# Causal masks of the prompt attention added by products of the rounded fp32 type in place of bf16 ones

## The chip, the cores and the metric

One core of a Trainium2 chip runs the whole kernel in one launch. The metric is the device time in microseconds, from which the median of several runs is taken; lower is better. The engines are TensorE (PE in the profile, its loads of stationary operands PEld), VectorE (DVE), ScalarE (ACT), GpSimd (POOL) and SyncE (SP), which issues most DMAs.

## The reference, cut to what matters

One layer of a decoder is computed for a prompt of 1024 tokens and for 8 sequences of 8 new tokens each, which attend to 8192 cached positions. A layer has gated linear attention, latent attention, an output projection, a gated MLP with a short convolution, and a gated embedding. The change lies in the prompt's part of the latent attention, with 8 heads of 96 (64 of values):

```python
def prompt_attention(q, k, v):           # q, k: (1, 1024, 8, 96); v: (1, 1024, 8, 64)
    ...
        s = jnp.einsum('bqhd,bkhd->bhqk', qi, k, preferred_element_type=jnp.float32) * MLA_SCALE
        qpos = start + jnp.arange(Q_BLOCK)
        s = jnp.where(kpos[None, :] <= qpos[:, None], s, NEG)      # NEG = -1e30
        pr = jax.nn.softmax(s, axis=-1)
        return jnp.einsum('bhqk,bkhd->bqhd', pr.astype(v.dtype), v)
```

## The kernel before, in words

Arithmetic is kept close to fp32 by splitting an operand into two of a rounded fp32 type (`F32R` in the code, `fp32r` or `f32` in the profile): a high part and the rest. A product is then the sum of three matmuls, high by high, high by low and low by high (`mm3`, L139 to L141).

Two streams of work share the core for the first half of the span. The cache stream (tiles `ks`, `csq`, `css`, `sn`, `phl`, `cpv`, `ctp`, `crp`, `chl`) reads the cached latents of the 8 sequences in blocks and does the new tokens' attention. The dense stream does the prompt: projections, linear attention, then `prompt_attention`, then the output projection. Generators yield shares of work, and a loop takes from the one or the other by a fixed table of paces. Within that, a scheduler sets the order of the instructions on each engine at build time from its own estimates of their durations, so a change of one instruction's type can move its neighbours; each engine then runs its list strictly in order. Buffers of a pool (three PSUM banks with the tag `d` here) are handed out in that order too.

`prompt_attention` goes through 16 rounds, one for each head `h` and half `g` of 512 queries. A round has two parts, and the second part of one round runs beside the first part of the next:

- `prepare` transposes and splits q and k of a head (`operands`, L1263), then `shifts` computes for each tile of 128 queries the scores against all keys up to the diagonal with the high parts alone (L1279, tile `t`), adds the mask to the 128 columns on the diagonal (L1281), and VectorE takes each row's maximum (L1282, `amx`). The negated maxima are transposed (L1292) into row 96 of `qh` and `ql`, which meets a row of ones in `kh`.
- `values` computes the scores transposed, 128 keys by up to 512 queries (tile `S`, three matmuls L1308, L1309, L1312), with a mask (L1311) where the keys are in the same half as the queries. There the tile has 512, 384, 256 or 128 columns. ScalarE takes the exponential (`p`), it is split (`ph`, `pl`, the rest on GpSimd, L1318), and three matmuls (L1323, L1324, L1326, at the end L1330) sum the values and the denominators in `o`.

A mask is a matmul: the identity as the stationary operand, a 128x128 matrix of 0 and -1e30 as the moving one, added to the scores that are in PSUM. `identb`, `maskq` and `maskk` are bf16, and are made once on GpSimd at the stage's start (L1240 to L1246). The 16 rounds have 4 tiles with a mask of each kind, so 64 matmuls at L1281 and 64 at L1311. A matmul with bf16 operands appears as a separate weight load and a matmul in the built program; one with operands of the rounded type is one instruction there, and the profile shows both halves in either case.

Of the kernel before, what the change touches and what calls it, by code (L numbers as in the profile page):

```python
# [8 lines left out]
F32 = mybir.dt.float32  # L9
F32R = mybir.dt.float32r  # L10
BF16 = mybir.dt.bfloat16
I32 = mybir.dt.int32
AF = mybir.ActivationFunctionType
ALU = mybir.AluOpType
# [4 lines left out]
P = 128  # L19
# [16 lines left out]
NEG = -1e30  # L36
# [8 lines left out]
def step_kernel(ctx: ExitStack, tc: tile.TileContext, A):  # L45
    nc = tc.nc
    pe, act, dve, pool, sp = nc.tensor, nc.scalar, nc.vector, nc.gpsimd, nc.sync
# [4 lines left out]
    def ctile(shape, dt, name):  # L52
        return const.tile(shape, dt, name=name, tag=name)
# [3 lines left out]
    ident = ctile([P, P], F32, "ident")  # L57
# [131 lines left out]
    def pat(kind):  # L189
        return psD.tile([P, 512], F32, tag="d", name=kind)  # L190
# [24 lines left out]
    for i in range(2):  # L215
        for s in range(2):
# [5 lines left out]
                       pattern=[[0, 8], [1, 8]], compare_op=ALU.is_ge, fill=NEG, base=0, channel_multiplier=-1)  # L222
# [1003 lines left out]
    def prompt_attention(ap):  # L1226
# [3 lines left out]
        def load(h):  # L1230
            ld = {}
            for nm, src, w in (("q", dq, 96), ("k", dk, 96), ("v", dv, 64)):
                t_ = ap.tile([P, NT, w], F32, tag="ld" + nm, name="ld" + nm, bufs=1)
                sp.dma_start(t_, src[:, h * w:(h + 1) * w].rearrange("(t p) c -> p t c", p=P))
                ld[nm] = t_
            return ld

        ld = {0: load(0)}
        identb = ap.tile([P, P], BF16, name="identb", tag="identb", bufs=1)
        pool.tensor_copy(identb, ident)  # L1240
        masks = []
        for nm, sg in (("maskq", 1), ("maskk", -1)):
            m = ap.tile([P, P], BF16, name=nm, tag=nm, bufs=1)
            pool.memset(m, 0.0)
            pool.affine_select(m, m, pattern=[[-sg, P]], compare_op=ALU.is_ge, fill=NEG, base=0, channel_multiplier=sg)
            masks.append(m)  # L1246
        maskq, maskk = masks
        qk, vo = [], []
# [20 lines left out]
        def shifts(h, g):  # L1269
            tr = qk[h % 2]  # L1270
            mx = ap.tile([P, 4, 2], F32, tag="amx", name="amx")
            for ii in range(4):
                i = 4 * g + ii
                qs = slice(i * P, (i + 1) * P)
                for j in range(g + 1):
                    kw = (ii + 1) * P if j == g else 512
                    S = pat("t")
                    k0 = j * 512
                    pe.matmul(S[:, 0:kw], tr["qh"][0:96, qs], tr["kh"][0:96, k0:k0 + kw], start=True, stop=j < g)  # L1279
                    if j == g:  # L1280
                        pe.matmul(S[:, kw - P:kw], identb, maskq, start=False, stop=True)  # L1281
                    dve.tensor_reduce(mx[:, ii, j:j + 1], S[:, 0:kw], AX.X, ALU.max, negate=True)  # L1282
                yield 0.06 * (i + 1)
            if g == 1:
                dve.tensor_tensor(mx[:, :, 0], mx[:, :, 0], mx[:, :, 1], ALU.min)
            return mx
# [9 lines left out]
        def values(h, g):  # L1296
            tr = qk[h % 2]
            v = vo[h % 2]
            o = pat("o")
            nj = 4 * g + 4  # L1300
            pls, q = {}, []
            for j in range(nj + 1):
                if j < nj:
                    c0 = max(0, j - 4 * g) * P
                    ks = slice(j * P, (j + 1) * P)
                    qs = slice(g * 512 + c0, g * 512 + 512)
                    S = pat("S")
                    pe.matmul(S[:, c0:], tr["kh"][:, ks], tr["qh"][:, qs], start=True, stop=False)  # L1308
                    pe.matmul(S[:, c0:], tr["kh"][:, ks], tr["ql"][:, qs], start=False, stop=False)  # L1309
                    if j >= 4 * g:  # L1310
                        pe.matmul(S[:, c0:c0 + P], identb, maskk, start=False, stop=False)  # L1311
                    pe.matmul(S[:, c0:], tr["kl"][:, ks], tr["qh"][:, qs], start=False, stop=True)  # L1312
                    p = ap.tile([P, 512], F32, tag="p", name="p", bufs=3)
                    ph = ap.tile([P, 512], F32R, tag="ph", name="ph", bufs=3)
                    pl = ap.tile([P, 512], F32R, tag="pl" if j else "pl0", name="pl", bufs=3 if j else 2)
                    act.activation(p[:, c0:], S[:, c0:], AF.Exp)
                    (dve.tensor_copy if j % 2 else act.copy)(ph[:, c0:], p[:, c0:])  # L1317
                    pool.tensor_tensor(pl[:, c0:], p[:, c0:], ph[:, c0:].bitcast(F32), ALU.subtract)  # L1318
                    q.append((j, c0, ph, pl))
                    yield 0.65  # L1320
                if j > 0:
                    jj, c0, ph, pl = q.pop(0)
                    pe.matmul(o[:, c0:], v[:, jj, 0:128], ph[:, c0:], start=jj == 0, stop=False)  # L1323
                    pe.matmul(o[0:64, c0:], v[:, jj, 128:192], ph[:, c0:], start=False, stop=False)  # L1324
                    if jj > 0:
                        pe.matmul(o[:, c0:], v[:, jj, 0:128], pl[:, c0:], start=False, stop=False)  # L1326
                    else:
                        pl0 = pl
                    yield 0.6
            pe.matmul(o, v[:, 0, 0:128], pl0, start=False, stop=True)  # L1330
            r = ap.tile([64, 512], F32, tag="ar", name="ar")
            act.activation(r, o[64:128, :], AF.Ln)
            act.activation(r, r, AF.Exp, scale=-1.0)
            dve.tensor_tensor(r, o[0:64, :], r, ALU.mult)
            sp.dma_start(doT[512 + h * 64:512 + (h + 1) * 64, g * 512:(g + 1) * 512], r)
            yield 0.2
# [10 lines left out]
        def prepare(n):  # L1347
            h, g = divmod(n, 2)
            if g == 0:
                yield from operands(h, ld.pop(h))  # L1350
                if h + 1 < H:
                    ld[h + 1] = load(h + 1)
            mx = yield from shifts(h, g)
            rows(h, g, mx)

        yield from prepare(0)
        for n in range(2 * H):
            yield from both(values(*divmod(n, 2)), prepare(n + 1) if n + 1 < 2 * H else iter(()))
# [904 lines left out]
```

## Time and profile before

| | |
|---|---|
| median of 3 runs | 2215.05 us (2214.86 to 2217.98) |
| span of the profiled execution, first to last instruction | 2211.1 us, mean granted clock 0.988 |
| own time of the profiled execution | not given apart; the runs' median lies 3.95 us over the span |
| PE busy | 2126.7 us, 96% |
| PEld, DVE, ACT, POOL busy | 87%, 75%, 62%, 56% |
| stage of the prompt attention | 645 to 1060 us of the span |

Busy times are unions of the instructions' spans. Matmuls are pipelined: a new one starts while the one before drains, so their durations overlap, and the throughput is read from the starts in the timeline. In the rows of groups the fields are line, engine, operation, out<-in, shape of the stationary operand, of the moving one, count, busy us and mean ns, and the idle time before them with what ended it.

### The profile page before, as it was taken

The page shows a single profiled execution, that of the slowest core. Times are in us where ns is not written, and L with a number is a line of the kernel's source. Part 1 is how long each engine was busy: PE and PEld are TensorE (multiplying, and loading weights), DVE is VectorE, ACT ScalarE, POOL GpSimd, SP SyncE. Part 2 cuts the span into 40 slices and gives each one's busy share as a digit, 9 for nine tenths or more (in the row PEclk, how much of TensorE's full clock was granted, in tenths as well). Part 3 has the DMA queues.
Part 4 walks back from the last instruction along what each step waited for, and adds up shares of the span by engine and source line. Part 5 has one row for each costly group of instructions (what it writes and reads, how often), then busy time and mean ns, then how long its engine had stood idle before and what let it go on. Part 6 is the DMA issues. An engine that isn't in the chain of part 4 may idle for free.

```text
span 2211.1 us, 38379 instructions
## 1 busy us (share of the span) xinstructions
PE 2126.7 (96%) x13460; PEld 1927.2 (87%) x13460; DVE 1668.4 (75%) x2551; ACT 1366.7 (62%) x3724; POOL 1233.9 (56%) x1330
## 2 busy tenths in 40 slices
PE   7999989999999999999999997999999999999999
PEld 6889978878888888887898875999999999888899
DVE  4775667467788888887888788888888886887642
ACT  5676766777778888887777766333333333534631
POOL 5675668576777777778455557756566562011100
PEclk9999999999999999999999998999999999999999
DMA  5343235412342222221522222332232325777321
GB/s 185 106 144 108 78 119 156 141 54 69 105 120 61 63 74 61 61 56 46 171 77 69 74 77 82 101 102 90 92 95 91 101 91 191 240 218 237 101 71 39
DMA packets 204418, 233.07 MB, mean 105 GB/s; under 512 B 42422, under 2 KB 146339, under 8 KB 204227
## 3 DMA queue, kind: packets, MB, share of 16 engines
q1 hardware_dynamic: 188259, 179.49, 26.0%
q0 software_dynamic: 14736, 46.67, 7.4%
q10 hardware_dynamic: 1232, 4.46, 0.5%
q8 instruction: 108, 1.77, 0.3%
q14 instruction: 83, 0.68, 0.1%
HBM read 188.00 MB, written 42.52 MB: 104 GB/s over the span
## 4 chain that ended last, share of the span: by engine, by line
PE 79%; DVE 7%; ACT 5%; DMA 3%; POOL 3%; issue 2%; SPq 0%; DVEq 0%; POOLq 0%; ACTq 0%
PE ps_gu L140 7%; PE ps_gu L141 7%; PE ps_gu L139 7%; PE ks L139 5%; PE ks L141 4%; PE ks L140 4%; PE ps_dn L140 3%; PE ps_dn L141 3%; PE ps_dn L139 3%; PE cpv L646 2%; PE ctp L522 2%; PE ps_lt L278 2%; PE ps_pj L139 2%; DVE css L565 1%; PE ps_pj L140 1%
## 5 line engine op out<-in xcount | busy, mean ns | idle before, releaser
L560 ACT ACTIVATE csq<-ks 128x256 f32<-128x256 f32 x1040 | 392.7, 400 | 91.1 <-PE ks L141 80.2
L565 DVE TENSOR_REDUCE css<-csq 128x16 f32<-128x1024 f32 (+1 forms) x264 | 315.7, 1196 | 61.2 <-ACT csq L560 58.2
L115 ACT CAST wh<-st 128x512 fp32r<-128x512 f32 x176 | 108.4, 619 | 189.0 <-PE ps_gu L140 168.7
L139 PE MATMUL ks<-mv0h,cTh 128*128 128x320 f32 (+1 forms) x520 | 171.0, 331 | 8.8 <-ACT sn L562 4.6
L139 PE MATMUL ks<-mv1h,cTh 128*128 128x320 f32 (+1 forms) x520 | 169.6, 328 | 7.8 <-ACT sn L562 3.5
L605 POOL TENSOR_TENSOR chl<-craw,chl 128x1024 fp32r<-128x1024 f32 x64 | 141.6, 2213 | 55.2 <-ACT chl L603 53.0
L140 PE MATMUL ks<-mv1l,cTh 128*128 128x320 f32 (+1 forms) x520 | 153.1, 296 | 0.0
L140 PE MATMUL ks<-mv0l,cTh 128*128 128x320 f32 (+1 forms) x520 | 152.0, 294 | 0.0
L141 PE MATMUL ks<-mv0h,cTl 128*128 128x320 f32 (+1 forms) x520 | 147.6, 297 | 0.9 <-DVE cTl L116 0.8
L141 PE MATMUL ks<-mv1h,cTl 128*128 128x320 f32 (+1 forms) x520 | 148.0, 298 | 0.1
L116 DVE TENSOR_TENSOR wl<-st,wh 128x512 fp32r<-128x512 f32 x132 | 119.0, 903 | 26.3 <-ACT wh L115 26.3
L631 POOL TENSOR_TENSOR phl<-sn,phl 128x512 fp32r<-128x512 f32 (+1 forms) x64 | 85.5, 1335 | 84.8 <-ACT phl L630 84.3
L116 POOL TENSOR_TENSOR wl<-st,wh 128x512 fp32r<-128x512 f32 x44 | 69.4, 1578 | 102.9 <-ACT wh L115 102.9
L140 PE MATMUL ps_dn<-o 128*128 128x512 f32 x308 | 120.1, 390 | 0.4 <-DVE o L116 0.4
L141 PE MATMUL ps_dn<-o 128*128 128x512 f32 x308 | 120.2, 390 | 0.0
L116 DVE TENSOR_TENSOR cTl<-ctp,cTh 128x512 fp32r<-128x512 f32 (+1 forms) x136 | 90.0, 662 | 37.8 <-ACT cTh L115 36.8
L139 PEld LDWEIGHTS ks<-mv0h,cTh 128*128 128x128 f32 x520 | 97.9, 188 | 23.2 <-ACT sn L562 9.4
L562 ACT COPY sn<-ks 128x64 f32<-128x64 f32 x520 | 116.7, 224 | 0.0
L139 PEld LDWEIGHTS ks<-mv1h,cTh 128*128 128x128 f32 x520 | 99.0, 190 | 20.1 <-ACT sn L562 7.9
L1318 POOL TENSOR_TENSOR pl<-p,ph 128x512 fp32r<-128x512 f32 (+1 forms) x96 | 97.5, 1020 | 30.3 <-DVE ph L1317 21.2
L139 PE MATMUL ps_dn<-o 128*128 128x512 f32 x308 | 112.1, 390 | 0.0
L141 PE MATMUL ps_gu<-xrh,wl 128*128 128x320 f32 x352 | 108.7, 309 | 0.0
(670 smaller groups left out, 7871.4 us busy)
## 6 DMA issues: line engine op xcount, KB each, us to landing
raw<-ds SPq DMA_DIRECT2D x77, 256.0 KB
raw<-ffn_w_down SPq DMA_DIRECT2D x66, 256.0 KB
stage<-w_in SPq DMA_DIRECT2D x48, 256.0 KB
st<-ffn_w_gate SPq DMA_DIRECT2D x44, 256.0 KB
st<-ffn_w_up SPq DMA_DIRECT2D x44, 256.0 KB
wr<-ffn_w_down SPq DMA_DIRECT2D x44, 256.0 KB
ds<-cv SPq DMA_DIRECT2D x21, 512.0 KB
oraw<-doT SPq DMA_DIRECT2D x16, 256.0 KB
```

The lines of the kernel that those rows point to most:

```text
L115: cast = act.copy(hi, src)
L116: res = (lo_eng or dve).tensor_tensor(lo, src, hi.bitcast(F32), ALU.subtract)
L139: pe.matmul(ps, ah, bh, start=first, stop=False)
L140: pe.matmul(ps, ah, bl, start=False, stop=False)
L141: return pe.matmul(ps, al, bh, start=False, stop=last)
L278: pe.matmul(ps, x, w, start=first, stop=last)
L560: act.activation(sq[:, f * 256:f * 256 + 256], ks[:, 0:256], AF.Square)
L562: act.copy(o.sn[:, g0 + i, :], ks[:, 256:320])
L565: dve.tensor_reduce(o.ss[:, g0 + i + 1 - n:g0 + i + 1, :].rearrange("p i h -> p (i h)"), sq2[:, :n].rearrange("p i (h n) -> p (i h) n", n= ...
L605: pool.tensor_tensor(ch[:, c0:c1, 128:256], src, ch[:, c0:c1, 0:128].bitcast(F32), ALU.subtract)
L631: pool.tensor_tensor(phl[:, :nt, 64:128], sb, phl[:, :nt, 0:64].bitcast(F32), ALU.subtract)
L1318: pool.tensor_tensor(pl[:, c0:], p[:, c0:], ph[:, c0:].bitcast(F32), ALU.subtract)
```

## The change

The identity and the two masks are kept in the rounded type. Since GpSimd's fill and selection write plain fp32, each mask is first made in a buffer `mraw` (one for both) and then cast. The two matmuls take `identr` in place of `identb`; nothing else is edited.

```diff
-        identb = ap.tile([P, P], BF16, name="identb", tag="identb", bufs=1)
-        pool.tensor_copy(identb, ident)
+        identr = ap.tile([P, P], F32R, name="identr", tag="identr", bufs=1)
+        pool.tensor_copy(identr, ident)
         masks = []
         for nm, sg in (("maskq", 1), ("maskk", -1)):
-            m = ap.tile([P, P], BF16, name=nm, tag=nm, bufs=1)
-            pool.memset(m, 0.0)
-            pool.affine_select(m, m, pattern=[[-sg, P]], compare_op=ALU.is_ge, fill=NEG, base=0, channel_multiplier=sg)
+            raw = ap.tile([P, P], F32, name="mraw", tag="mraw", bufs=1)
+            m = ap.tile([P, P], F32R, name=nm, tag=nm, bufs=1)
+            pool.memset(raw, 0.0)
+            pool.affine_select(raw, raw, pattern=[[-sg, P]], compare_op=ALU.is_ge, fill=NEG, base=0, channel_multiplier=sg)
+            pool.tensor_copy(m, raw)
             masks.append(m)
...
-                        pe.matmul(S[:, kw - P:kw], identb, maskq, start=False, stop=True)
+                        pe.matmul(S[:, kw - P:kw], identr, maskq, start=False, stop=True)
...
-                        pe.matmul(S[:, c0:c0 + P], identb, maskk, start=False, stop=False)
+                        pe.matmul(S[:, c0:c0 + P], identr, maskk, start=False, stop=False)
```

Lines behind the masks' making stand two further down in the changed kernel (L1281 is L1283, L1311 is L1313, L1312 is L1314). On every engine the order differs only within the stage of the prompt attention; behind it the same rows follow with other buffer numbers. Three places show how. On GpSimd at the start of the stage, before (the matching rows from the selections on):

```order
L473 DMA craw<-cache_ckv,idx 128x1024 x2
L1245 AFFINE_SELECT maskq<-maskq 128x128
L1245 AFFINE_SELECT maskk<-maskk 128x128
L592 TENSOR_TENSOR sn<-sn,cy 128x512
L116 TENSOR_TENSOR vo_9440<-ldv,vo_9440 128x8x64
L631 TENSOR_TENSOR phl<-sn,phl 128x9x64
L594 TENSOR_TENSOR sn<-sn,sr 128x512
L605 TENSOR_TENSOR chl<-craw,chl 128x8x128
```

and now:

```order
L1246 AFFINE_SELECT mraw<-mraw 128x128
L592 TENSOR_TENSOR sn<-sn,cy 128x512
L116 TENSOR_TENSOR vo_9444<-ldv,vo_9444 128x8x64
L631 TENSOR_TENSOR phl<-sn,phl 128x9x64
L1247 CAST maskq<-mraw 128x128
L594 TENSOR_TENSOR sn<-sn,sr 128x512
L1245 MEMSET mraw 128x128
L1246 AFFINE_SELECT mraw<-mraw 128x128
L1247 CAST maskk<-mraw 128x128
L605 TENSOR_TENSOR chl<-craw,chl 128x8x128
```

The first mask is finished behind `phl`, the second behind the `sn` that follows it, and `chl` comes behind both. On TensorE, at the first round, where `cpv` is the cache stream's product that needs `phl`, before:

```order
L646 MATMUL cpv<-chl,phl 128x258 x9
L1308 MATMUL S<-qh_9436,kh_9438 128x512
L1279 MATMUL t<-kh_9438,qh_9436 128x512
L1309 MATMUL S<-ql_9437,kh_9438 128x512
L1311 LDWEIGHTS identb
L1311 MATMUL S<-maskk,identb 128x128
L1312 MATMUL S<-qh_9436,kl_9439 128x512
```

and now:

```order
L646 MATMUL cpv<-chl,phl 128x258 x9
L1283 MATMUL t<-maskq,identr 128x128 x3
L1281 MATMUL t<-kh_9442,qh_9440 128x512
L1283 MATMUL t<-maskq,identr 128x128
L1294 MATMUL t<-ident,amx 1x128 x3
L522 MATMUL ctp<-ident,craw 128x128 x4
L500 MATMUL crp<-ident,krraw 128x128 x2
L1294 MATMUL t<-ident,amx 1x128
```

The masks of the first four score tiles, which stood ahead of `cpv`, now stand behind it, and the first tile of values starts later by these rows and six products of the cache stream. On TensorE near the stage's end, at the last but one `cpv` there, before:

```order
L1323 MATMUL o<-ph,vo_9448 128x512
L1324 MATMUL o<-ph,vo_9448 64x512
L1279 MATMUL t<-kh_9446,qh_9444 128x512
L1323 MATMUL o<-ph,vo_9448 128x384
L1324 MATMUL o<-ph,vo_9448 64x384
L1279 MATMUL t<-kh_9446,qh_9444 128x384
L1281 LDWEIGHTS identb
L1281 MATMUL t<-maskq,identb 128x128
L646 MATMUL cpv<-chl,phl 128x258 x8
L500 MATMUL crp<-ident,krraw 128x128 x2
```

and now:

```order
L1281 MATMUL t<-kh_9450,qh_9448 128x512
L1281 MATMUL t<-kh_9450,qh_9448 128x256
L1283 MATMUL t<-maskq,identr 128x128
L646 MATMUL cpv<-chl,phl 128x258 x8
L500 MATMUL crp<-ident,krraw 128x128 x2
L1325 MATMUL o<-ph,vo_9452 128x512
L1326 MATMUL o<-ph,vo_9452 64x512
L1325 MATMUL o<-ph,vo_9452 128x384
L1326 MATMUL o<-ph,vo_9452 64x384
L1281 MATMUL t<-kh_9450,qh_9448 128x512
L1281 MATMUL t<-kh_9450,qh_9448 128x384
L1283 MATMUL t<-maskq,identr 128x128
```

The `cpv` moved ahead of four products of values and a score tile.

## Prediction

> **What bounds the kernel now.** I read the page first, then the stretch in which the two masks are used, then the matmul lines by shape, and last the matmul timeline around single masks.
>
> ```profile
> PE 2126.7 (96%) x13460; PEld 1927.2 (87%) x13460; DVE 1668.4 (75%) x2551; ACT 1366.7 (62%) x3724; POOL 1233.9 (56%) x1330
> ...
> PE 79%; DVE 7%; ACT 5%; DMA 3%; POOL 3%; issue 2%; SPq 0%; DVEq 0%; POOLq 0%; ACTq 0%
> ```
> TensorE is busy for 96% of the span and holds 79% of the chain that ended last. Below, "slot" is the time from the start of one matmul to the start of the next: the durations overlap, so only slots add up.
>
> ```profile
> 645.00:1060.00 415.00, 401.40 (x2737) 350.28 (x2735) 340.20 (x552) 355.87 (x1053) 310.24 (x316) 0.99 0.24 68
> ...
> 1020.00:1030.00 10.00, 7.59 (x41) 5.94 (x40) 6.57 (x12) 4.51 (x10) 7.81 (x13) 0.85 0.06 14
> 1030.00:1040.00 10.00, 8.78 (x45) 7.04 (x45) 4.57 (x10) 7.15 (x15) 7.63 (x8) 0.84 0.26 66
> ```
> The columns are length, then busy time of PE, PEld, DVE, ACT, POOL, then the granted clock. In the stage of the masks TensorE idles for 415.00 - 401.40 = 13.6 us; 3.6 us of it lie in the 20 us at the stage's end, where the clock falls to 0.85 too. So a nanosecond on TensorE in this stage is nearly a nanosecond of time, and no other engine is near full.
>
> ```profile
> L1281 PE MATMUL t<-maskq,identb 128*128 128x128 bf16 x64 | 14.4, 230 | 0.0
> ...
> L1326 PEld LDWEIGHTS o<-pl,vo 128*128 128x128 f32 x80 | 15.4, 193 | 1.6 <-POOL pl L1318 0.7
> ...
> L1311 PEld LDWEIGHTS <-identb 128*128 128x128 bf16 x64 | 6.3, 98 | 7.6 <-issue 6.9
> ```
> There are 64 masks of scores (L1281) and 64 of values (L1311). A stationary operand of 128x128 in the rounded type loads in 193 ns, the bf16 identity in 98 ns.
>
> **The change, part by part.**
>
> *A mask between wide products.* What it costs in bf16:
>
> ```profile
> 699.10 0.40 PE L1309 MATMUL S<-ql,kh 97*128 97x512 f32 x1
> 699.34 0.23 PE L1311 MATMUL S<-maskk,identb 128*128 128x128 bf16 x1
> 699.38 0.48 PE L1312 MATMUL S<-qh,kl 97*128 97x512 f32 x1
> 699.70 0.28 PE L139 MATMUL csr<-qbd1h,kTh 128*128 128x256 f32 x1
> ```
> The mask's own slot is 0.04 us, but the wide product after it takes 0.32 us. Without a mask ahead the same line takes 0.23, in the next rows, which also hold the nearest thing to the new mask: L1326, a narrow product of the rounded type with a full stationary operand, between two wide ones.
>
> ```profile
> 889.02 0.39 PE L1312 MATMUL S<-qh,kl 97*128 97x512 f32 x1
> 889.25 0.23 PE L1326 MATMUL o<-pl,vo 128*128 128x128 f32 x1
> 889.31 0.45 PE L1330 MATMUL o<-pl,vo 128*128 128x512 f32 x1
> 889.60 0.28 PE L139 MATMUL ks<-mv0h,cTh 128*128 128x256 f32 x1
> ```
> So bf16 costs 0.04 + (0.32 - 0.23) = 0.13 us. The rounded narrow product costs its slot of 0.06 and delays L1330 to 0.29, so 0.06 + (0.29 - 0.23) = 0.12. In both types the product behind the narrow one waits for its own stationary operand, which can't load early under so short a cover. I take 0.015 us less for each mask (the rows are printed to 0.01, so between 0 and 0.02). Of the 128 masks 96 stand so: all but those of the 128-wide tiles.
>
> *A mask among narrow products.* Each of the 16 rounds (8 heads, 2 halves) has one tile of scores and one of values that is 128 wide; here the last of values, in bf16:
>
> ```profile
> 1047.31 0.23 PE L1308 MATMUL S<-qh,kh 97*128 97x128 f32 x1
> 1047.37 0.27 PE L1309 MATMUL S<-ql,kh 97*128 97x128 f32 x1
> 1047.49 0.23 PE L1311 MATMUL S<-maskk,identb 128*128 128x128 bf16 x1
> 1047.53 0.31 PE L1312 MATMUL S<-qh,kl 97*128 97x128 f32 x1
> 1047.67 0.45 PE L1326 MATMUL o<-pl,vo 128*128 128x512 f32 x1
> 1047.96 0.39 PE L1323 MATMUL o<-ph,vo 128*128 128x512 f32 x1
> ```
> From 1047.31 to 1047.96 are 0.65 us; less the wide slot of 0.23, four narrow products cost 0.42. In the rounded type alone such a row runs so:
>
> ```profile
> 1019.91 0.22 PE L1323 MATMUL o<-ph,vo 128*128 128x128 f32 x1
> 1019.97 0.22 PE L1324 MATMUL o<-ph,vo 128*64 128x128 f32 x1
> 1020.03 0.27 PE L1326 MATMUL o<-pl,vo 128*128 128x128 f32 x1
> 1020.14 0.45 PE L1330 MATMUL o<-pl,vo 128*128 128x512 f32 x1
> 1020.42 0.22 PE L1279 MATMUL t<-kh,qh 96*128 96x128 f32 x1
> ```
> L1326, whose successor needs a full stationary operand and whose predecessor was narrow, has a slot of 0.11. Four in a row are then 0.06 + 3 x 0.11 for the slots and 0.06 for the delay of the wide one behind, 0.45 in all: 0.03 us more than with the bf16 mask. I take 0.03 for all 32 such masks.
>
> Sum on TensorE: 96 x -0.015 + 32 x 0.03 = -1.44 + 0.96 = -0.5 us. The bounds: at the lower end the delay of the product behind vanishes and a mask costs its slot alone, 0.06 for 0.13, 128 x -0.07 = -9.0 us. At the upper end the slower load is not covered at all, 193 - 98 = 95 ns, 128 x 0.095 = +12.2 us. I stay at -0.5, since L1326 is the same shape, type and place as the new mask.
>
> The Trainium skill speaks against the change here: "TensorE: Matmul & The Clock Gate", section "Weight-path perf modes — Fast Weight Load (FWL) and DoubleRow", gives the fast load of stationary operands to 128-wide ones that aren't fp32, by a factor of about two as measured there. The trace agrees with that factor, 193 against 98 ns. Its section "LDWEIGHTS (loading the stationary operand)" gives columns over 1.2 for the plain load, 107 ns for 128; were each of the 128 masks to cost that in full, an estimate is 13.7 us where my rows give 128 x 0.12 = 15.4 for the wide case, and 128 x 0.13 = 16.6 for bf16 in the same rows: by the page the sum would be 13.7 - 16.6 = -2.9 us, by the rows -0.5.
>
> *Building the masks on POOL*, once:
>
> ```profile
> 647.07 0.50 POOL L1240 CAST identb<-ident 128x128 bf16<-128x128 f32 x1
> 647.52 0.20 POOL L1244 MEMSET maskq<- 128x128 bf16 x1
> ...
> 651.14 0.53 POOL L1255 MEMSET vo<- 128x512 f32 x1
> ...
> 656.52 0.31 POOL L1245 TENSOR_SCALAR_AFFINE_SELECT maskq<-maskq 128x128 bf16<-128x128 bf16 x1
> 656.79 0.29 POOL L1245 TENSOR_SCALAR_AFFINE_SELECT maskk<-maskk 128x128 bf16<-128x128 bf16 x1
> ...
> 659.35 1.40 POOL L631 TENSOR_TENSOR phl<-sn,phl 128x576 fp32r<-128x576 f32 x1
> 660.72 1.28 POOL L594 TENSOR_TENSOR sn<-sn,sr 128x512 f32<-128x512 f32 x1
> 663.24 2.19 POOL L605 TENSOR_TENSOR chl<-craw,chl 128x1024 fp32r<-128x1024 f32 x1 [1.25 <-PE S L1312]
> ```
> Two casts are added, 2 x 0.50 by L1240, whose size they have. The fills and the two selections move from 2 to 4 bytes: a fill between 0.20 and 0.53, a selection between 0.31 and twice that. Together +1.0 to +2.3 us; I take 1.3, since the cast between these types takes 0.50 whatever comes out. One buffer (mraw) serves both masks, so the second's fill waits for the first's cast on the same engine. Because maskk is now built behind phl, phl itself comes 0.20 + 0.29, about 0.5 us, earlier. Then follow maskq's cast, L594 (1.28) and maskk's three instructions (about 1.1), ahead of L605, which idled 1.25 us before it. That idle time hides them; if it is gone, L605 starts up to 0.6 us late, and who waits for it is the next block's cpv product, many matmuls later. In the new order the first scores masks stand behind cpv and the first value mask some thirty matmuls behind that, about 4 us by their slots, so TensorE waits for neither. Cost: nothing.
>
> *The moved rows.* The order in front of this text shows that TensorE now runs cpv first and the masks of the first tiles after it, and that values of the first round start about 3 us of matmuls later. The counts of matmuls are the same, and behind the stage the order is the same again but for buffer names. The 13.6 us of idle time above are what a new order can shrink or grow; the pieces that stand in a row are under 2 us each except at the end. No row says which way, so I put 0, with 4 us either side.
>
> The sum: 0 + 0 - 0.5 = -0.5 us. The profiled execution has a span of 2211.1, 3.95 us under the median of 2215.05 of the runs, which is what lies around it; 2210.6 + 3.95 = 2214.5 us. A change within 0.2% (4.4 us) can hardly be told from none here.
>
> **The rivals.**
> - *The load of the rounded identity is exposed* (slower). Place: every mask; price up to +12.2 us, so 2227. It decides where the queue takes the load only once the matmul ahead has ended. For it: 193 against 98 ns. Against it: the slot of 0.06 at 889.25. From a third of the price on, 4 us, it would show. 0.06.
> - *The delay behind the mask belongs to the change of type and not to the load* (faster). Then the product behind a rounded mask has no delay: -9.0 us, 2206. Against it: L1330 with 0.29 and no change of type ahead of it. 0.05.
> - *The new order closes idle time* (faster). At the stage's end TensorE lost 3.6 us to idling and, with a clock of 0.85 over 20 us, up to 3 more. If the cache stream, which ran ahead at the start, and attention end closer together, about 7 us go: 2207.5. For it: the first maximum no longer waits early for a mask. Against it: in the order the last cpv still stands among products of attention, with no latent products around. 0.18.
> - *The new order opens idle time* (slower). Attention starts some 3 us of matmuls later and must be caught up; with too little of the cache stream left beside its last round, the hole at the end grows by that and by one block's wait of about 2: 2220. For it: three score tiles now hold all three buffers until their masks come. 0.13.
>
> **How the numbers follow.** Forecast 0.58, the rivals 0.06, 0.05, 0.18 and 0.13. That gives faster 0.23, within 0.2% 0.58, slower 0.19. The forecast's own range, 4 us either side for the order, is 2210.5 to 2218.5. The range for all takes in most of both order rivals, 2207.5 to 2220.5, and leaves out the two rivals on the load and the outer halves of these.
>
> **What would show it.** In the changed profile: slots of 0.06 for a mask between wide products and 0.29 for a 512-wide product behind it; L1314 behind a 128-wide mask near 0.11; loads of identr near 190 ns; the casts of maskq and maskk at 0.50; TensorE idle for 10 to 17 us in the stage. The prediction is wrong if mask slots are well above 0.06 with the delay behind them unchanged, if that delay is gone, or if idle time at the stage's end (the 20 us with the lower clock) moves by over 4 us.

## The result, and the profile after

| | before | after |
|---|---|---|
| median | 2215.45 us (2213.76 to 2219.06, 7 runs) | 2223.98 us (2222.17 to 2229.53, 7 runs) |
| ratio of after to before | | 1.0041, 95% interval 1.0031 to 1.0051 |
| span of the profiled execution | 2211.1 us | 2221.6 us |

The change costs 8.5 us. The forecast was 2214.5 us with a range up to 2220.5; the result lies 3.5 us above it.

The page of the changed kernel, busy times and the chain that ended last:

```profile
PE 2129.2 (96%) x13460; PEld 1936.8 (87%) x13460; DVE 1661.2 (75%) x2551; ACT 1368.2 (62%) x3724; POOL 1231.9 (55%) x1332
...
PE 78%; DVE 9%; ACT 5%; DMA 3%; POOL 3%; issue 2%; SPq 0%; DVEq 0%; POOLq 0%; ACTq 0%
```

Nothing stands out: TensorE is still the bound, only VectorE's share of the chain has grown from 7% to 9%. So the stage of the masks comes next, with the columns as in the prediction (busy PE, PEld, DVE, ACT, POOL, granted clock):

```profile
645.00:1060.00 415.00, 397.42 (x2695) 355.06 (x2693) 332.21 (x546) 349.71 (x1024) 309.88 (x314) 0.99 0.24 67
1020.00:1030.00 10.00, 9.90 (x68) 8.70 (x67) 7.01 (x14) 8.64 (x30) 7.31 (x13) 1.00 0.23 67
1030.00:1040.00 10.00, 8.24 (x48) 6.42 (x48) 8.14 (x15) 5.33 (x11) 9.74 (x11) 1.00 0.11 27
...
1040.00:1050.00 10.00, 8.28 (x34) 6.74 (x34) 3.58 (x8) 6.00 (x11) 6.62 (x7) 0.66 0.17 53
```

and the last of these windows before:

```profile
1040.00:1050.00 10.00, 10.00 (x60) 8.12 (x60) 6.01 (x8) 6.78 (x14) 9.38 (x9) 0.97 0.11 29
```

From 645 to 1060 TensorE idles for 415.00 - 397.42 = 17.6 us in place of 13.6. The hole at the stage's end is no bigger, it only comes later: 1.8 + 1.7 = 3.5 us between 1030 and 1050, where before had 3.6 between 1020 and 1040. The same goes for the granted clock: from 1020 to 1050 it falls short of full by 3.4 us in either kernel (before 1.5 + 1.6 + 0.3, after 3.4 in the last window alone). The end of the mask work tells how much is lost. The tile `maskk` before (first row) and after (second), with least, median and largest duration in ns and the first and last start:

```profile
L1311 PE MATMUL S<-maskk,identb x64: 230/231/330, 662.7 to 1047.5; 128*128 128x128 bf16 x64
```
```profile
L1313 PE MATMUL S<-maskk,identr x64: 222/226/307, 668.7 to 1056.9; 128*128 128x128 f32 x64
```

The first value mask comes 6.0 us later than before, the last 9.4. The stage itself began 1.2 us later (the identity's cast on GpSimd at 648.25 and 647.07), so some 8 us arise in it. To see where, I cut the stage at 200 us behind that cast, before (first fence) and after:

```profile
647.07:847.07 200.00, 194.01 (x1346) 169.92 (x1344) 167.58 (x277) 174.85 (x525) 150.93 (x155) 1.00 0.28 79
847.07:1047.07 200.00, 193.70 (x1297) 168.19 (x1298) 161.72 (x264) 168.07 (x487) 151.82 (x153) 0.98 0.20 56
```
```profile
648.25:848.25 200.00, 190.13 (x1311) 171.38 (x1310) 165.65 (x271) 169.62 (x512) 148.46 (x154) 0.99 0.27 75
848.25:1048.25 200.00, 192.44 (x1294) 171.03 (x1293) 158.78 (x266) 168.68 (x489) 148.63 (x152) 0.99 0.21 59
```

In the first 200 us TensorE's idle time grows from 6.0 to 9.9 us, in the second from 6.3 to 7.6. The first mask products on TensorE show what differs at the start, before and after:

```profile
656.88 0.33 PE L1281 MATMUL t<-maskq,identb 128*128 128x128 bf16 x3
...
660.80 1.35 PE L646 MATMUL cpv<-chl,phl 128*128 128x258 f32 x9 [0.49 <-POOL phl L631]
662.71 0.23 PE L1311 MATMUL S<-maskk,identb 128*128 128x128 bf16 x1
```
```profile
661.47 1.35 PE L646 MATMUL cpv<-chl,phl 128*128 128x258 f32 x9 [0.90 <-POOL phl L631]
662.66 0.45 PE L1283 MATMUL t<-maskq,identr 128*128 128x128 f32 x3
...
668.72 0.23 PE L1313 MATMUL S<-maskk,identr 128*128 128x128 f32 x1
```

and GpSimd, after, why:

```profile
657.44 0.31 POOL L1246 TENSOR_SCALAR_AFFINE_SELECT mraw<-mraw 128x128 f32<-128x128 f32 x1
657.72 1.09 POOL L592 TENSOR_TENSOR sn<-sn,cy 128x512 f32<-128x512 f32 x1
658.76 1.29 POOL L116 TENSOR_TENSOR vo<-ldv,vo 128x512 fp32r<-128x512 f32 x1
660.01 1.41 POOL L631 TENSOR_TENSOR phl<-sn,phl 128x576 fp32r<-128x576 f32 x1
661.36 0.29 POOL L1247 CAST maskq<-mraw 128x128 fp32r<-128x128 f32 x1
661.61 1.28 POOL L594 TENSOR_TENSOR sn<-sn,sr 128x512 f32<-128x512 f32 x1
662.84 0.20 POOL L1245 MEMSET mraw<- 128x128 f32 x1
663.11 0.29 POOL L1246 TENSOR_SCALAR_AFFINE_SELECT mraw<-mraw 128x128 f32<-128x128 f32 x1
663.47 0.29 POOL L1247 CAST maskk<-mraw 128x128 fp32r<-128x128 f32 x1
```

Counted from the identity's cast, the first mask product stands at 662.66 - 648.25 = 14.4 us, before at 9.8. The select is done at 657.75, but three other rows stand between it and the cast. The masks are finished at 661.65 and 663.76; before, both were finished at 657.08. Counted from the identity's cast that is 3.4 and 5.5 us later.

### The profile page after: what moved, and what is told of

Its sections match the earlier page's. It is cut to its first block, busy times and chain, and to the rows that moved or that the text cites. A ratio compares the mean times of both kernels' runs of the same rounds, so it can differ in the third digit from the quotient of the medians.

```text
span 2221.6 us, 38390 instructions
## 1 busy us (share of the span) xinstructions
PE 2129.2 (96%) x13460; PEld 1936.8 (87%) x13460; DVE 1661.2 (75%) x2551; ACT 1368.2 (62%) x3724; POOL 1231.9 (55%) x1332
## 4 chain that ended last, share of the span: by engine, by line
PE 78%; DVE 9%; ACT 5%; DMA 3%; POOL 3%; issue 2%; SPq 0%; DVEq 0%; POOLq 0%; ACTq 0%
PE ps_gu L140 7%; PE ps_gu L141 7%; PE ps_gu L139 7%; PE ks L139 5%; PE ks L141 4%; PE ks L140 4%; PE ps_dn L140 3%; PE ps_dn L141 3%; PE ps_dn L139 3%; PE cpv L646 2%; PE ctp L522 2%; DVE css L565 2%; PE ps_pj L139 2%; PE ps_lt L278 2%; PE ps_pj L140 1%
## 5 line engine op out<-in xcount | busy, mean ns | idle before, releaser
L1320 POOL TENSOR_TENSOR pl<-p,ph 128x512 fp32r<-128x512 f32 (+2 forms) x96 | 97.0, 1016 | 28.8 <-ACT ph L1319 18.7
L139 PE MATMUL ps_gu<-xrh,wh 128*128 128x320 f32 x352 | 108.6, 309 | 0.9 <-ACT xrh L115 0.9
```

The source lines that it names most:

```text
L139: pe.matmul(ps, ah, bh, start=first, stop=False)
```

## The experiments

Theory at first: the products cost what the prediction says, and the time is lost by the new order of rows. Rival: the rounded products are dearer than their slots show. Later, with the order found guilty: is it bad by chance, by single waits that can be named, or because the masks come late? Each ratio is to the kernel before, run beside it on the same chip, with a 95% interval.

Three settings were varied. The type of identity and masks; how a mask is made (`direct`: the select writes the mask; `raw`: one fp32 buffer for both, then casts; `raw2`: a buffer each, then casts); and whose order is held. To hold an order, the kernel was scheduled once in the other form, and in the final build each row was made to stand behind its predecessor there, without a semaphore. The edits below are written for a kernel with these settings in it; before is `('bf16', 'direct')`, after `('f32r', 'raw')`:

```python
for a, b in zip(row, row[1:]):
    tc.add_manual_dep(by[b], by[a].name, NoSync)
```

### Products apart from order

**Rounded products, all engines in the order of before.**

```diff
-CFG = ('f32r', 'raw')
+CFG = ('f32r', 'raw2'); ORDER_OF = ('bf16', 'direct')
```

> The changed kernel's products (rounded fp32 identity and masks) with every engine's instruction order held to that of the kernel before; the two masks are made in two buffers of their own and cast. Theory 'the order lost the time': the products alone cost what the rows gave, -0.5 us, so about 2215 (2213 to 2217), with TensorE's idle time in the stage as before. Rival 'the products or the making of the masks lost it': about 2224, as the changed kernel.

Measured: 0.9989 (0.9979 to 0.9999), 2.4 us faster, with 0.2 to 4.7 us in the interval. The rounded products with their casts cost nothing; the forecast's -0.5 us is inside.

**bf16 products, all engines in the order of after.**

```diff
-CFG = ('bf16', 'direct')
+CFG = ('bf16', 'direct'); ORDER_OF = ('f32r', 'raw')
```

> The kernel before's bf16 products with every engine's order held to that of the changed kernel; the masks are made without casts. Theory 'the order lost the time': about 2224 (2221 to 2226), with GpSimd's rests of the exponentials waited for by TensorE for some 5 us in the stage. Rival 'products': about 2215.

Measured: 1.0034 (1.0021 to 1.0047). No rounded product and no cast, and 7.5 us of the 8.5 are there (4.7 to 10.4). By the two profiles TensorE's 13460 matmuls stand in exactly the order of after. The order carries the loss.

### What made the order

**bf16 products, masks through one fp32 buffer and casts, scheduler free.**

```diff
-CFG = ('bf16', 'direct')
+CFG = ('bf16', 'raw')
```

> bf16 products, but the masks made as in the changed kernel (one fp32 buffer, cast to bf16); the scheduler is free, and its order differs from both kernels' in about 1700 and 1400 of 13094 matmuls. Theory 'any new order of the stage is worth some microseconds either way, this one happened to be bad': between 2209 and 2224, not to be told beforehand. Rival 'late masks at the stage's start lose the time': about 2224, since the masks are late here too.

Measured: 1.0038 (1.0022 to 1.0053). The casts, with the order that the scheduler makes for them, bring a like loss, with products as before.

**The changed kernel with a buffer for each mask, scheduler free.**

```diff
-raw = ap.tile([P, P], F32, name="mraw", tag="mraw", bufs=1)
+raw = ap.tile([P, P], F32, name="mraw", tag="mraw" + nm, bufs=1)
```

> Rounded products as in the changed kernel, but a buffer for each mask's making, so the second needn't wait for the first; the scheduler is free, and about 1060 of 13094 matmuls stand otherwise than before. Theory 'the order': between 2209 and 2224, nearer to before (2216) as its order is nearer. Rival 'products': about 2224.

Measured: 1.0037 (1.0019 to 1.0055). The shared buffer isn't the cause.

**The changed kernel, TensorE alone in the order of before.**

```diff
-CFG = ('f32r', 'raw')
+CFG = ('f32r', 'raw'); ORDER_OF = ('bf16', 'direct'); ENGINES = ['PE']
```

> The changed kernel word for word (one buffer for both masks), with TensorE's order alone held to that of before; the scheduler sets the other engines' orders around it, and they differ from before's in only 9 to 12 rows each. Theory 'the place of the products of the two streams on TensorE lost the time': as the run with every order held, 2215 to 2217 (ratio 0.998 to 1.000). Rival 'the late second mask and the casts on GpSimd lost it': about 1.003 to 1.004.

Measured: 1.0022 (1.0013 to 1.0031), half the loss. The old order asks for the mask before GpSimd has it. TensorE's largest wait in the first 55 us:

```profile
PE t L1298 <- POOL maskq L1262: 3.2, 1, 3.2
```

So the late mask is paid in the old order too, there as a wait.

**Rounded, a buffer each, GpSimd alone in the order of before.**

```diff
-CFG = ('f32r', 'raw2')
+CFG = ('f32r', 'raw2'); ORDER_OF = ('bf16', 'direct'); ENGINES = ['Pool']
```

> The changed kernel's products, a buffer for each mask, GpSimd's order alone held to that of before; TensorE's differs from before's in about 1770 matmuls. Theory 'GpSimd's rests of the exponentials come late in the new order, for which TensorE waited 5.3 us': that wait goes and the ratio is near 1.000. Rival 'the order on TensorE': ratio 1.003 to 1.004, with other waits in its place.

Measured: 1.0181 (1.0167 to 1.0194), against about 1.000 expected: a miss. TensorE's order came out 1770 matmuls from that of before. About half of the time is lost behind the stage: the dense stream's products of L1434 (tile `ps_dn`) begin 20.7 us later than before (1083.0 and 1062.3) and end 42.3 later (1370.5 and 1328.2). Why the lists that the scheduler made around GpSimd's come out so badly wasn't followed up; the run says nothing on the masks.

**Rounded, a buffer each, all orders held up to 745 us only, free behind.**

```diff
+row = row[:int(hi * len(row))]  # hi of each engine: what stands ahead of 745 us
```

> The changed kernel's products, a buffer for each mask, all engines' orders held to before's up to about 745 us of the span, free behind; there 1093 matmuls stand otherwise. Theory 'the late start of the first round lost the time': gone, ratio 0.999 to 1.000. Rival 'the loss is spread over the stage': ratio 1.001 to 1.003, since three quarters of the stage are free.

Measured: 1.0004 (0.9994 to 1.0013), though 1093 matmuls behind stand elsewhere than before. With one free order behind 745 us, the loss is gone: what it needs is decided in the stage's first 100 us.

### Single waits, or chance

The list of TensorE's waits in the stage has one entry that has grown much, that for `pl` (engine, line, waited for, total us, times, longest). After:

```profile
PE o L1328 <- POOL pl L1320: 5.3, 4, 2.6
...
PE cpv L646 <- POOL phl L631: 1.8, 3, 0.9
```

and before:

```profile
PE cpv L646 <- POOL phl L631: 1.3, 2, 0.8
...
PE o L1326 <- POOL pl L1318: 0.4, 1, 0.4
```

Its longest piece on GpSimd and TensorE: the `pl` of 745 us stands behind rows of the cache stream that began late, by a wait for a transfer.

```profile
740.26 0.79 POOL L490 CAST qbd1h<-qr 32x64 fp32r<-32x64 f32 x3 [3.30 <-DMA craw<-cache_ckv,idx]
...
745.05 0.45 POOL L1320 TENSOR_TENSOR pl<-p,ph 128x128 fp32r<-128x128 f32 x1
```
```profile
745.56 0.48 PE L1328 MATMUL o<-pl,vo 128*128 128x128 f32 x1 [2.55 <-POOL pl L1320]
```

**The changed kernel in its own order, four `pl` moved ahead.**

```diff
+MOVES = [(15, 4), (49, 3), (82, 3), (83, 3)]  # (which pl, rows earlier on GpSimd)
```

> Changed kernel, its own order held on every engine, but four GpSimd rows (the low parts pl of four score tiles) stand earlier: the one of 745 us by 4 rows, the one of 886 us by 3, the two of 1030 us by 3, so that each starts as soon as its input is there and does not stand behind GpSimd's casts and products of the decode rows. TensorE waited 2.55, 1.06 and 1.17 us for them. If these waits are the loss in itself, the time falls by 4.8 us, a ratio to the kernel before of about 1.002; if TensorE, once freed, meets the next late input instead, the ratio stays at 1.004 and other waits in the stage grow by as much.

Measured: 1.0045 (1.0031 to 1.0059): nothing gained. The waits in the same stretch:

```profile
PE cpv L654 <- POOL phl L639: 3.7, 3, 2.0
...
PE o L1346 <- POOL pl L1338: 0.3, 1, 0.3
```

The wait for `pl` went from 5.3 to 0.3 us, that for `phl`, which the moved rows now delay, grew from 1.8 to 3.7. TensorE's idle time from 645 to 1060 fell only from 17.6 to 16.0 us, and the last value mask still starts 409.0 us behind the identity's cast (408.6 in after). Taking these waits away doesn't take the loss away.

**bf16 kernel, another pace of the streams.** The table of paces shares the work between the two streams; a small step makes the scheduler find another order.

```diff
-PACE = [1.41, 1.088, 1.601, 1.168, 1.142, 0.708, 1.035, 1.027]
+PACE = [1.41, 1.088, 1.601, 1.168, 1.142, 0.708, 1.03, 1.027]
```

> The kernel before with nothing changed but one pace of the table, 1.035 to 1.03, for the stage of the prompt attention: the same instructions, of which 643 matmuls stand elsewhere. Theory 'the order of before is a good one for the stage and other orders of it are worse by some microseconds': ratio 1.001 to 1.004. Rival 'orders scatter evenly around before's': as likely under as over 1, and 'only orders with casts or wide estimates of the products are bad': 1.000.

Measured: 0.9979 (0.997 to 0.9988), faster, where the theory expected a worse time: a miss. The order of before isn't a best one; 643 matmuls elsewhere can also help.

**Rounded products in that order.**

```diff
-CFG = ('f32r', 'raw')
+CFG = ('f32r', 'raw2'); ORDER_OF = ('bf16', 'direct'), both at the pace 1.03
```

> Rounded products with a buffer per mask, every engine's order held to that of the nudged old kernel (0.9979). If order and products are worth what the runs so far say and add up (0.9979 and 0.9989), the ratio is 0.997, and this is the fastest of all versions; if products and order depend on each other, it lies anywhere between 0.998 and 1.002.

Measured: 0.9993 (0.9984 to 1.0002). Gains of order and products don't add up: here rounded products are 0.14% slower than bf16 in the same order, in the first run they were 0.11% faster. The two runs and their bf16 partners ran on different chips; taken together the products have no sign that these runs can tell.

**The changed kernel at the paces 1.03 and 1.02.**

```diff
-PACE = [1.41, 1.088, 1.601, 1.168, 1.142, 0.708, 1.035, 1.027]
+PACE = [1.41, 1.088, 1.601, 1.168, 1.142, 0.708, 1.03, 1.027]   # then 1.02
```

> The changed kernel word for word, except the pace of part 6 in the due times, 1.03 in place of 1.035: the products are the same, 651 matmuls stand elsewhere than in the changed kernel. If the loss belongs to the one order that the scheduler happened to find, this order gives another time, anywhere between 0.997 and 1.004, and the idle time of TensorE in the stage moves with it; if it belongs to the rounded products or to the masks' later readiness, the ratio stays at 1.004.

> As the run before it, with 1.02 (681 matmuls stand elsewhere than in the changed kernel). Same two forecasts: anywhere between 0.997 and 1.004 if the order alone decides, 1.004 if the products or the masks' readiness do.

Measured: 1.0019 (1.001 to 1.0028) and 1.0017 (1.0008 to 1.0026). So some of the 0.4% belongs to the one order; but no order that the scheduler found for masks with casts has come near 1.000 yet.

### Late masks

**Rounded products without casts.** The select can write the rounded type itself, so the reason given for the casts, that it writes plain fp32, doesn't hold.

```diff
-raw = ap.tile([P, P], F32, name="mraw", tag="mraw", bufs=1)
 m = ap.tile([P, P], F32R, name=nm, tag=nm, bufs=1)
+raw = m.bitcast(F32)
 pool.memset(raw, 0.0)
-pool.affine_select(raw, raw, ...)
-pool.tensor_copy(m, raw)
+pool.affine_select(m, raw, ...)
```

> Rounded products, scheduler free, but no casts: the causal select writes the rounded fp32 mask itself, so that both masks stand on GpSimd where the bf16 ones stood (two fills, then two selects one behind the other) and are ready some 5 us sooner than in the changed kernel. 1108 matmuls stand elsewhere than in the kernel before. If the casts' late masks are what makes the scheduler's order a bad one, the ratio falls to that of the kernel before or below (0.997 to 1.001); if the rounded products do it, or any new order costs 0.4%, it stays at 1.004.

Measured: 0.9994 (0.9985 to 1.0003). The loss is gone, with 1108 matmuls elsewhere than before. The masks are ready early:

```profile
655.55 0.31 POOL L1246 TENSOR_SCALAR_AFFINE_SELECT maskq<-maskq 128x128 fp32r<-128x128 f32 x1
655.82 0.30 POOL L1246 TENSOR_SCALAR_AFFINE_SELECT maskk<-maskk 128x128 fp32r<-128x128 f32 x1
656.09 1.07 POOL L592 TENSOR_TENSOR sn<-sn,cy 128x512 f32<-128x512 f32 x1
```

**The same at the pace 1.03, and bf16 with casts at the pace 1.03.** The edits are the ones shown.

> As the run before it, with the pace of part 6 at 1.03. If the late masks decide, 0.997 to 1.001, as with bf16 masks and this pace (0.9979); if the order is chance alone, anywhere between 0.997 and 1.004.

> The bf16 products with masks that go through an fp32 buffer and two casts (1.0038 at the old pace), with the pace of part 6 at 1.03. If the late masks decide, the ratio stays above that of the kernel before (1.001 to 1.004, as the changed kernel at this pace, 1.0019); if the order is chance alone, anywhere between 0.997 and 1.004.

Measured: 0.9998 (0.9989 to 1.0007) and 1.0044 (1.003 to 1.0057). Now the table is full, and one factor, the casts, sorts it:

| | masks by select alone | masks by select and cast |
|---|---|---|
| bf16, pace 1.035 | 1 (before) | 1.0038 |
| bf16, pace 1.03 | 0.9979 | 1.0044 |
| rounded, pace 1.035 | 0.9994 | 1.0041 (after) |
| rounded, pace 1.03 | 0.9998 | 1.0019 |

**Casts kept near the selects.** One piece of GpSimd's order is held: select, cast, select, cast, then the next `sn`.

```diff
-CFG = ('f32r', 'raw2')
+CFG = ('f32r', 'raw2'); ORDER_OF = ('bf16', 'direct'); ENGINES = ['Pool']; SPAN = ('affmaskq', 7)
```

> Rounded products with casts and a buffer per mask, scheduler free, except that on GpSimd the two selects and two casts are held in one piece ahead of the next decode row (sn<-sn,cy), which without that goes ahead of the casts. The casts stay, only their place changes; 390 matmuls stand elsewhere than in the kernel without casts. If the late masks decide, the ratio is that of the kernel without casts (0.9994), 0.998 to 1.0015; if the casts as such or the rounded products do, or chance, it is about 1.004 as with the same kernel unheld (1.0037).

Measured: 1.0026 (1.0013 to 1.0038). Between the two forecasts. `phl` slipped in between the first select and its cast, and TensorE's first mask product still stood 14.2 us behind the identity's cast, so the run didn't bring about what it was meant to.

**Casts early.** The held piece is longer (12 rows), so that `phl` too stands behind the casts.

```diff
-SPAN = ('affmaskq', 7)
+SPAN = ('affmaskq', 12)
```

> As the last run (rounded products, casts, a buffer per mask, scheduler free), but select, cast, select, cast are now held ahead of all the decode rows that stand behind the masks in the kernel before (phl too); TensorE's order comes out 58 matmuls from that of the rounded kernel without casts (0.9994). If the masks' late place decides, the ratio is 0.998 to 1.001; if the casts as such do, 1.0026 to 1.004.

**No casts, late selects.** The rounded kernel without casts, with its selects held where the changed kernel has its casts.

```diff
+# held piece of after's GpSimd order, its casts replaced by the selects
+row = [(e, "aff" + k[1][4:]) if str(k[1]).startswith("cast") else k for k in row]
```

> The rounded kernel without casts (0.9994), but on GpSimd the two selects are held where the changed kernel's casts stand: the first behind three decode rows, the second behind one more. No product and no cast is added, only the masks come some 4 to 6 us later; the scheduler is free in all else. If the late place decides, the ratio rises to that of the changed kernel (1.002 to 1.0045); if the casts as such do, it stays within 0.998 and 1.001.

Measured: casts early 1.0026 (1.0015 to 1.0036), late selects 1.0033 (1.0021 to 1.0046). GpSimd and the stage's first 200 us in the second:

```profile
658.44 1.44 POOL L636 TENSOR_TENSOR phl<-sn,phl 128x576 fp32r<-128x576 f32 x1
659.83 0.29 POOL L1260 TENSOR_SCALAR_AFFINE_SELECT maskq<-maskq 128x128 fp32r<-128x128 f32 x1
...
661.36 0.28 POOL L1260 TENSOR_SCALAR_AFFINE_SELECT maskk<-maskk 128x128 fp32r<-128x128 f32 x1
```
```profile
646.74:846.74 200.00, 191.86 (x1326) 173.41 (x1325) 163.74 (x273) 171.16 (x517) 150.25 (x153) 0.99 0.27 77
```

Late masks, without a cast and with no other edit, bring the loss: 1.0033 against 0.9994, and 8.1 us of idle time against 6.5. The order that the scheduler makes around them belongs to it: by the two profiles some 1900 of TensorE's 13460 matmuls stand otherwise. The converse fails: early masks with casts don't restore the time, though the same casts cost nothing in the orders held to before's (0.9989, 1.0004). So by the two forecasts neither place nor casts are the whole cause. No run holds such a piece without moving anything, so what the hold itself is worth in these three runs isn't known.

In the kernel with early casts TensorE's order is only 58 matmuls from the one without casts; by the profiles about 44 of them stand in the first 37 us behind the identity's cast, the rest at the stage's end and behind it. Ahead of the masks a product stands 3.9 us later than in the kernel without casts (a `ks` at 658.00 and 654.07), behind them 9.6 us later (699.61 and 690.04); at 1000 us the distance is still 9.5. So 5.7 us arise in some 35 us. Part of them are waits (first 55 us behind the identity's cast):

```profile
PE t L1296 <- DVE amx L1299: 1.7, 1, 1.7
PE ks L144 <- ACT cTh L120: 1.3, 1, 1.3
PE S L1325 <- ACT qh L120: 0.9, 1, 0.9
```

In the one without casts the first and the third are 0, the second is the same, and there is a wait of `S` for `amx` of 1.1. Another part is the granted clock, here from 20 to 30 us behind the identity's cast, with early casts (first row) and without casts:

```profile
670.03:680.03 10.00, 8.81 (x41) 7.94 (x42) 4.73 (x13) 4.17 (x14) 8.86 (x10) 0.66 0.29 92
```
```profile
666.10:676.10 10.00, 10.00 (x73) 9.49 (x73) 8.15 (x17) 7.78 (x27) 8.36 (x9) 1.00 0.34 93
```

These 10 us hold 1.2 us of idle time more, and the clock of 0.66 takes 3.4. So the opening of the stage is the sensitive place, and the masks' date is one of the things that upset it. That in the execution with early casts the clock fell there because of the waits isn't shown: in the profile of the rounded products in the order of before it is 0.70 from 10 to 20 us, with 0.85 us of idle time, where before has 1.00 with 1.15.

### All runs side by side

TensorE's idle time, each 200 us counted from the identity's cast (windows as shown above), and the start of the first mask product from the same point:

| kernel | first mask, us | idle 0 to 200 | idle 200 to 400 | ratio |
|---|---|---|---|---|
| before | 9.8 | 6.0 | 6.3 | 1 |
| bf16, pace 1.03 | 10.5 | 5.9 | 5.9 | 0.9979 |
| rounded in the order of before | 10.2 | 5.7 | 6.0 | 0.9989 |
| rounded in the order of pace 1.03 | 10.2 | 5.8 | 5.8 | 0.9993 |
| order held to 745 us | 10.2 | 6.3 | 8.3 | 1.0004 |
| rounded, no casts | 10.4 | 6.5 | 8.3 | 0.9994 |
| rounded, no casts, pace 1.03 | 10.1 | 6.4 | 7.5 | 0.9998 |
| after | 14.4 | 9.9 | 7.6 | 1.0041 |
| after, buffer each | 14.9 | 10.8 | 6.2 | 1.0037 |
| after, pace 1.03 | 14.5 | 9.4 | 6.3 | 1.0019 |
| after, pace 1.02 | 14.5 | 9.4 | 6.5 | 1.0017 |
| after, four rows ahead | 14.4 | 8.9 | 6.9 | 1.0045 |
| bf16 with casts | 14.4 | 11.4 | 8.9 | 1.0038 |
| bf16 with casts, pace 1.03 | 14.5 | 11.3 | 7.7 | 1.0044 |
| bf16 in the order of after | 14.4 | 10.1 | 7.5 | 1.0034 |
| TensorE's order alone held | 13.4 | 8.2 | 7.1 | 1.0022 |
| casts near the selects | 14.2 | 7.7 | 7.7 | 1.0026 |
| casts early | 10.3 | 8.5 | 8.1 | 1.0026 |
| no casts, late selects | 14.5 | 8.1 | 8.8 | 1.0033 |

All kernels with at most 6.5 us in the first 200 have a ratio up to 1.0004, all with 7.7 or more have 1.0017 or more. Within the slow group the idle time doesn't rank them: 7.7 goes with 1.0026, 9.4 with 1.0017. The second 200 us tell the two groups hardly apart (5.8 to 8.3 and 6.2 to 8.9). The run that held GpSimd's order alone is left out.

The granted clock can be part of a ratio. In every kernel of the slow group but one its mean over the runs is a little lower than in those of before beside them, as far as it is on record: 0.984 against 0.986 for the changed kernel at the pace 1.03, 0.982 against 0.985 for bf16 in the order of after. Over the 119 runs of before in the experiments, 0.001 less clock went with about 1.3 us more, so by this estimate up to some 3 us of a loss can go with it, in the changed kernel at the paces 1.03 and 1.02 more than half. It isn't the whole: the late selects lose 0.33% with 0.986 against 0.985.

## Why the prediction was wrong

**Products: right.** Slots, between wide products and at a narrow one, after:

```profile
707.60 0.40 PE L1311 MATMUL S<-ql,kh 97*128 97x512 f32 x1
707.84 0.23 PE L1313 MATMUL S<-maskk,identr 128*128 128x128 f32 x1
707.90 0.45 PE L1314 MATMUL S<-qh,kl 97*128 97x512 f32 x1
708.18 0.28 PE L139 MATMUL ks<-mv1h,cTh 128*128 128x256 f32 x1
```
```profile
1041.47 0.28 PE L1311 MATMUL S<-ql,kh 97*128 97x128 f32 x1
1041.58 0.28 PE L1313 MATMUL S<-maskk,identr 128*128 128x128 f32 x1
1041.69 0.27 PE L1314 MATMUL S<-qh,kl 97*128 97x128 f32 x1
```

The mask has 0.06, the wide product behind it 0.28 (0.29 forecast), narrow ones 0.11, as forecast. Over the 16 value tiles of each width, a mask and the product behind it take 0.346 us at the median where the tile has 512 columns (0.362 before), 0.223 where it has 128 (0.185 before): -0.016 and +0.038 for the -0.015 and +0.03 of the prediction. The load of the identity takes what was said (about 190 ns), beside other work:

```profile
L1313 PEld LDWEIGHTS S<-maskk,identr 128*128 128x128 f32 x64 | 12.1, 189 | 0.6
```

So both rivals on the load are out. The term of -0.5 us stands within the first experiment's interval; in the order of the pace 1.03, where the rounded products came out 0.14% slower, it isn't borne out, so its sign stays open. The estimate of -2.9 us by the load's figure in the Trainium skill ("TensorE: Matmul & The Clock Gate", section "LDWEIGHTS (loading the stationary operand)") would lie within the first interval as well; no run here tells these two apart.

**Masks on GpSimd: the waits right, the conclusion not.** `phl`, and `cpv` behind it, came 0.5 us earlier as forecast (`cpv` 13.2 us behind the identity's cast, 13.7 before); the casts took 0.29, not 0.50; TensorE waits for no mask, and the list of its waits has none. From that the prediction concluded "Cost: nothing". But that nobody waits was a property of an order that the scheduler had made around the late mask. In TensorE's order of before the same lateness is a wait of 3.2 us. The step asked whether the new order waits for the masks, and took the order itself for free.

**The moved rows: the step that failed.** "No row says which way, so I put 0, with 4 us either side." Measured: 1.0034 in the order of after with everything else as before, +7.5 us for a term that was put at 0 (4.7 to 10.4, all of it outside the 4 us). Late masks and the order made around them gave 1.0033 against 0.9994, +8.7 us. Sign and size could not be read from the idle time of before. That attention starts later was seen and put at 3 us; the first value mask came 4.8 us later, counted from the identity's cast (20.5 against 15.6), and the step priced it as if a gain were as likely.

**The rival "the new order opens idle time"** named what happened, and had 0.13, but by another path and too low. Its price, 2220, was the hole at the end grown by 3 us and a block's wait of 2; the hole only moved, from 1020 to 1040 to 1030 to 1050, and the idle time opened at the other end of the stage, 3.9 us in the first 200. The forecast's own sign, 10 to 17 us of idle time in the stage, was passed (17.6).

**The sum.** The 3.95 us between span and median were taken for what lies around the span. In the seven runs of the changed kernel the time is 1.7 to 2.3 us over the span, so some 2 us of the 3.95 were scatter between runs. The forecast doesn't hang on it: 2215.05 - 0.5 gives the same 2214.5.

**What stays open.** Of the 8.2 us that arise between the identity's cast and the last value mask, 5.1 are idle time of TensorE (408.6 - 391.2 = 17.4 us against 400.4 - 388.1 = 12.3). Another piece is the granted clock. Right behind the wait for `pl` at 745 us, in which TensorE is busy for 1.35 of 3.41 us, it is low for a while:

```profile
741.65:745.06 3.41, 1.35 (x9) 0.88 (x7) 0.00 (x0) 3.36 (x10) 3.12 (x6) 1.00 0.01 2
745.06:748.48 3.42, 2.92 (x12) 2.73 (x13) 1.97 (x3) 1.41 (x4) 3.42 (x6) 0.57 0.00 0
```

From 738.25 to 758.25 the clock falls short by 1.8 us (0.86 and 0.96 in 10 us each), where it is 1.00 in the same windows of before. Together that is about 7 of the 8.2 us; the rest isn't tied to rows. Why the scheduler's orders around late masks or casts came out worse each time, and not at times better, wasn't settled: the largest waits could be moved but not removed, and early casts cost 0.26% with a different list of waits.

## What to carry to other kernels

Where a scheduler sets the order, an added instruction on an engine with time to spare isn't priced by its duration alone. Two casts of 0.29 us, which the scheduler put behind other rows, made the masks 3 to 6 us late, and the four orders that it found around them for the two product types and the two first paces were 0.2 to 0.4% slower than before; writing the final type in the select took that back. The date is part of the price and not all of it, since casts held early still cost 0.26%. That nobody waits in the new order is no proof of a free edit, since the order was made around it; hold the order fixed, and then edit the readiness alone, to tell the two apart. A change of type and the re-ordering that it brings are separate terms, and the second has a size: with the scheduler free, here between -0.2% and +0.4%.

## What the runs showed that I had not expected

- GpSimd's cast of a 128x128 tile from fp32 took 0.29 us for the masks, to the rounded type and to bf16 alike, but 0.49 for the identity in the same kernels. Why isn't known.
- Holding one engine's list while the others are scheduled anew can be far worse than either order: 1.0181 with GpSimd's held.
- With the pace of one stage changed by 0.5%, the bf16 kernel gained 0.21% (0.12 to 0.30) and the changed one 0.22% of its 0.41: at this size an order is worth more than the type of 128 products.
